# A two-layer decoder trunk on one core: fewer VectorE steps in GELU, softmax coefficients and gate norm, and another plan of the order

## The chip, the core and the metric

The kernel runs on one core of one Trainium2 chip. The core has a matrix engine (TensorE, PE in the profile, its weight loads PEld), three engines for elementwise work (VectorE = DVE, ScalarE = ACT, GpSimd = POOL), a queue that starts transfers (SyncE = SP), and 16 DMA engines between the chip's memory (HBM) and the core's own. The metric is the device time of one launch in microseconds, the median of several runs; lower is better.

## What is computed

One sequence of 512 tokens, width 1024, passes through two layers. Each mixes the tokens by three head groups side by side and adds a feed-forward; all modulated by a conditioning vector c:

```python
for l in range(DEPTH):
    mod = (silu(c) @ w_ada[l] + b_ada[l])[:, None, :]
    sh1, sc1, g1, sh2, sc2, g2 = jnp.split(mod, 6, axis=-1)
    h = x * (1.0 + sc1) + sh1
    (hq, hf, hi, hg, nq, kcm, vcm, ksl, vsl, kwn, vwn, ngt, gu, gv) = jnp.split(h @ w_in[l], cuts, axis=-1)
    o_h = hgrn2(...)          # a gated recurrence in chunks of 64
    o_n = nsa(...)            # sparse attention: compressed, selected and window part
    o_g = gmlp(gu, gv, ...)   # gelu(gu) * (tril(w_s) @ LN(gelu(gv)) + b_s)
    mix = jnp.concatenate([o_h, o_n, o_g], axis=-1) @ w_o[l]
    x = layer_norm(DN_ALPHA * x + (1.0 + g1) * mix, ln1_w[l], ln1_b[l])
    h = x * (1.0 + sc2) + sh2
    y = jnp.square(jax.nn.relu(h @ w_ff1[l])) @ w_ff2[l]
    x = layer_norm(DN_ALPHA * x + (1.0 + g2) * y, ln2_w[l], ln2_b[l])
# attention: out = g0 * softmax(cmp) @ v_cmp + g1 * softmax(slc) @ v_slc + g2 * softmax(win) @ v_win
# gelu(x) = 0.5 x (1 + tanh(sqrt(2/pi) (x + 0.044715 x^3)))
```

## The kernel before

Matrix products keep float32 accuracy by splitting each operand into a high part and a residual: `whi` and `wlo` of a weight piece `wraw`, `hT` and `aT` in pairs of the activations, three matmuls for one product. The residual `wlo` can be made by VectorE or GpSimd.

The program goes through eight stages. Layer 0's mixing lasts from 0 to about 347 us: the conditioning products (`adaw`, summed on VectorE into `adacc`, turned into columns by `ada_cols` or rows), the input projections, the recurrence (`hq`, `hog`, states `hst`), the compression of keys and values (`KV` copies, a small network with GELU into `chid`), the attention in eight units of 128 queries and four heads, the gMLP, the output projection. Then layer 0's feed-forward to about 727 us, layer 1's mixing to about 1021, its feed-forward to about 1387, and a tail with the last layer norm.

In an attention unit (`att_unit`) each of four heads has three score parts. VectorE takes the negated row maximum (`amax`), ScalarE the exponential with its row sum, VectorE the reciprocal of the sums times the gates (`acoef`, 128 rows by four heads by three parts), then the probabilities `P` are scaled (`scale_rows`: GpSimd, VectorE or ScalarE), transposed on TensorE into the bank `aps`, and copied as a high part and a residual `PT`. The projections of `hi`, `hg`, `gv` and `gu` run between the units. `gelu2` is used by the compression (four tiles of 62 rows, source in PSUM) and by `ev_gu` and `ev_gv` (eight tiles of 128x256 in each). `ev_gv` also does the gMLP's norm, with statistics `gst`, `gmv` and rows of weights `gnw`; its two halves go to `gmv[k]`. `final_rows` makes the last residual: `rt` from a bank, `y` = `rt` + `base`, then statistics `lnst`, and at the end `xs`, the normed rows.

The code does not run in the order in which it is written. Every call on `V`, `A`, `G`, `PE` or `SP` makes an operation in a `Plan`, some with alternatives: `vg` names VectorE first and GpSimd second, `gv` the other way. `schedule` then places all operations by a list scheduler (`place_all`): at each step an engine takes the ready operation of the best priority. Durations come from `cost`, distances between engines from `LAT`. An alternative that is not the first is taken only when the operation has been ready for `ALT_WAIT` ns. After each round, `latest(order)` works the priorities out of the latest starts of the order just found; the order with the earliest modelled end is emitted. Since operations are emitted from one line, that line carries all the instructions in the profile, and tiles tell them apart.

Of the kernel before, what the change touches and what calls it, by code (L numbers as in the profile page):

```python
# [161 lines left out]
ALT_WAIT = 500.0  # L162
# [5 lines left out]
ROUNDS = 6  # L168
# [28 lines left out]
class Plan:  # L197
# [158 lines left out]
    def schedule(self, rounds=ROUNDS):  # L356
# [16 lines left out]
        for r in range(rounds):  # L373
            if r:
                self.latest(order)
                reset()
            order = self.place_all()
            end = max(o.end for o, _ in order)
            if best is None or end < best[0]:
                best = (end, order, [(vt, vt.slot) for vt in tiles])  # L380
# [43 lines left out]
    def place_all(self):  # L424
# [90 lines left out]
        while n_left:  # L515
            best = None
            for e in T:
# [14 lines left out]
                for r in sorted(ready[e])[:200]:  # L532
# [4 lines left out]
                    if r[2] and t < o.ready + ALT_WAIT:  # L537
                        fut = min(fut, max(st, o.ready + ALT_WAIT))
# [12 lines left out]
                if cand is None:  # L551
                    for r in pend[e]:
# [5 lines left out]
                        fut = min(fut, max(r[0] + (ALT_WAIT if r[2] else 0), slot_time(o, r[0]), bank_time(o, e),  # L558
# [13 lines left out]
            c = self.cost(*alt)  # L572
# [112 lines left out]
def trunk(ctx: ExitStack, tc: tile.TileContext, I, out, depth=L):  # L685
# [362 lines left out]
    def ada_cols(l, v, c0, acc, dst):  # L1048

        nb = acc.shape[1] // 128  # L1050
        p = ps()[:, :nb * 128]
# [111 lines left out]
    def layer(l, yn, xd, sb1, rest, mods):  # L1163
# [235 lines left out]
        def gelu2(dst, src, n, tag):  # L1399
# [4 lines left out]
            A.activation(a, src, AF.Square)  # L1404
            V.tensor_scalar(a, a, 0.044715, 1.0, op0=OP.mult, op1=OP.add)
            (V.tensor_mul if src.vt.cls == "ps" else lambda *z: vg("tensor_mul", *z))(a, a, src)
# [100 lines left out]
        def ev_gv(j, p):  # L1507
# [9 lines left out]
            V.tensor_scalar(ge, ge, mv[:, 0:1], mv[:, 2:3], op0=OP.subtract, op1=OP.mult)  # L1517
            vg("tensor_mul", ge, ge, gnw[:, 0])
            for k in range(2):
                vg("tensor_add", gmv[k][:, j], ge[:, k * 128:(k + 1) * 128], gnw[:, 1, k * 128:(k + 1) * 128])  # L1520
# [12 lines left out]
        def att_unit(g, i):  # L1533
# [5 lines left out]
            for h in range(4):  # L1539
# [26 lines left out]
                srcs = (p0[:, n0 - n:n0], p1[:, :n], pcm)  # L1566
                for m in range(3):
                    V.tensor_reduce(nm[:, h, m:m + 1], srcs[m], axis=AX.X, op=OP.max, negate=True)
                dsts = (Pt[0][:, :n], Pt[1][:, :n], Pc[:, h])
# [4 lines left out]
            cf = small([128, 4, 3], "acoef", 4)  # L1574
            V.reciprocal(cf, sm)
            gt = gates[:, i, 12 * g:12 * g + 12].rearrange("p (h m) -> p h m", m=3)
            V.tensor_mul(cf[:, :, 0:1], cf[:, :, 0:1], gt[:, :, 1:2])
            V.tensor_mul(cf[:, :, 1:2], cf[:, :, 1:2], gt[:, :, 2:3])
            V.tensor_mul(cf[:, :, 2:3], cf[:, :, 2:3], gt[:, :, 0:1])
            if i == 0:  # L1580
                V.tensor_scalar(cf[:, :, 2:3], cf[:, :, 2:3], cvalid, None, op0=OP.mult)
            for h in range(4):
                for m in range(2):
                    scale_rows(Ps[h][m][:, :n], cf[:, h, m:m + 1])
# [381 lines left out]
```

## Time and profile before

| | us |
|---|---|
| median of 3 runs | 1399.25 |
| lowest, highest | 1399.09, 1402.97 |
| the profiled execution | 1398.26 |
| its span, first to last instruction | 1396.5 |
| TensorE busy | 1346.9 (96%) |
| VectorE busy | 1051.6 (75%) |
| ScalarE busy | 580.2 (42%) |
| GpSimd busy | 428.5 (31%) |

Times of single instructions are of the profiled execution. Busy time of an engine counts its instructions; its idle time before an instruction is put down to what ended it. A row that stands for several instructions gives their count (x16) and the mean of one. The granted clock of TensorE is 0.993 of full speed in the mean of the span.

### The profile page before, as it was taken

The page shows a single profiled execution, that of the slowest core. Times are in us where ns is not written, and L with a number is a line of the kernel's source. Part 1 is how long each engine was busy: PE and PEld are TensorE (multiplying, and loading weights), DVE is VectorE, ACT ScalarE, POOL GpSimd, SP SyncE. Part 2 cuts the span into 40 slices and gives each one's busy share as a digit, 9 for nine tenths or more (in the row PEclk, how much of TensorE's full clock was granted, in tenths as well). Part 3 has the DMA queues.
Part 4 walks back from the last instruction along what each step waited for, and adds up shares of the span by engine and source line. Part 5 has one row for each costly group of instructions (what it writes and reads, how often), then busy time and mean ns, then how long its engine had stood idle before and what let it go on. Part 6 is the DMA issues. An engine that isn't in the chain of part 4 may idle for free.

```text
span 1396.5 us, 21252 instructions
## 1 busy us (share of the span) xinstructions
PE 1346.9 (96%) x7339; PEld 1124.7 (81%) x7339; DVE 1051.6 (75%) x2242; ACT 580.2 (42%) x1570; POOL 428.5 (31%) x623
## 2 busy tenths in 40 slices
PE   5998999989999999999999999999999999999997
PEld 4887788868888888888889878888788888888886
DVE  8997799989786495585888957988995448634567
ACT  6567587862343133211325467876333102210121
POOL 6685345582210000000224632336530000000024
PEclk9999999999999999999999999999999999999999
DMA  9734634136564294283503351112643235413431
GB/s 308 231 99 123 208 105 143 46 108 199 169 207 156 83 320 140 92 290 123 166 1 108 110 174 44 31 46 91 212 133 100 90 96 170 149 39 109 125 113 61
DMA packets 119844, 185.67 MB, mean 133 GB/s; under 512 B 9796, under 2 KB 47160, under 8 KB 119736
## 3 DMA queue, kind: packets, MB, share of 16 engines
q1 hardware_dynamic: 119736, 184.31, 41.9%
q8 instruction: 58, 0.95, 0.3%
q14 instruction: 50, 0.41, 0.1%
HBM read 175.89 MB, written 8.39 MB: 132 GB/s over the span
## 4 chain that ended last, share of the span: by engine, by line
PE 75%; DVE 12%; ACT 4%; DMA 4%; issue 2%; POOL 2%; SPq 1%; POOLq 0%; DVEq 0%; ACTq 0%
PE acc L681 64%; PE aps L681 7%; PE ps L681 5%; DMA adaw<-in_w_ada_dram 2%; DVE adacc L681 1%; DMA adaq<-in_w_ada_dram 1%; DVE amax L681 1%; DMA wraw<-in_w_in_dram 1%; DVE ge L681 1%; ACT P L681 1%; ACT KV L681 1%; DVE PT L681 1%; SPq L681 1%; DVE r L681 1%; DVE rt L681 1%
## 5 line engine op out<-in xcount | busy, mean ns | idle before, releaser
L681 PE MATMUL acc<-hT,whi 128*128 128x512 f32 (+1 forms) x1296 | 414.7, 374 | 3.8 <-ACT hT L681 3.5
L681 POOL TENSOR_TENSOR wlo<-wraw,whi 128x256 fp32r<-128x256 f32 (+2 forms) x133 | 152.6, 1158 | 612.9 <-ACT whi L681 533.3
L681 PE MATMUL acc<-whi,aT 128*128 128x512 f32 x896 | 325.1, 394 | 0.0
L681 PEld LDWEIGHTS acc<-hT,whi 128*128 128x128 f32 x1296 | 235.4, 190 | 49.4 <-ACT hT L681 4.3
L681 PE MATMUL acc<-hT,wlo 128*128 128x512 f32 (+1 forms) x648 | 239.6, 372 | 0.1
L681 PE MATMUL acc<-whi,hT 128*128 128x256 f32 (+2 forms) x1024 | 230.2, 308 | 3.3 <-ACT KV L681 2.5
L681 PEld LDWEIGHTS acc<-whi,aT 128*128 128x128 f32 x896 | 168.2, 188 | 39.5
L681 DVE TENSOR_TENSOR wlo<-wraw,whi 128x512 fp32r<-128x512 f32 (+2 forms) x267 | 182.7, 700 | 13.6 <-ACT whi L681 6.4
L681 ACT ACTIVATE ffa<-acc 128x512 f32<-128x512 f32 x64 | 38.1, 596 | 372.1 <-PE acc L681 371.1
L681 ACT ACTIVATE whi<-wraw 128x512 fp32r<-128x512 f32 (+2 forms) x253 | 131.3, 556 | 120.1 <-DMA wraw<-in_w_ff_dram 71.8
L681 PEld LDWEIGHTS acc<-whi,hT 128*128 128x128 f32 x1024 | 169.7, 191 | 11.2 <-ACT KV L681 3.5
L681 PE MATMUL acc<-wlo,aT 128*128 128x512 f32 x448 | 176.8, 395 | 0.0
L681 PE MATMUL acc<-wlo,hT 128*128 128x256 f32 (+2 forms) x512 | 156.2, 306 | 0.4 <-DVE wlo L681 0.4
L681 DVE TENSOR_TENSOR ffs<-ffa 128x512 f32<-128x512 f32 x64 | 46.7, 732 | 141.4 <-ACT ffa L681 141.3
L681 PEld LDWEIGHTS acc<-hT,wlo 128*128 128x128 f32 x648 | 123.1, 190 | 23.0 <-DVE wlo L681 0.5
L681 DVE SCALAR_TENSOR_TENSOR adacc<-adaw,silc,adacc 128x512 f32<-128x512 f32 x140 | 113.8, 823 | 15.4 <-DMA adaw<-in_w_ada_dram 13.8
L681 PEld LDWEIGHTS acc<-wlo,hT 128*128 128x128 f32 x512 | 97.6, 191 | 3.4 <-DVE wlo L681 0.6
L681 PEld LDWEIGHTS acc<-wlo,aT 128*128 128x128 f32 x448 | 84.1, 188 | 19.6
L681 ACT ACTIVATE P<-aps,amax 128x128 f32<-128x128 f32 (+3 forms) x128 | 66.9, 530 | 14.3 <-DVE amax L681 12.2
L681 DVE TENSOR_REDUCE amax<-aps 128x1 f32<-128x32 f32 (+4 forms) x192 | 65.4, 379 | 8.5 <-PE aps L681 7.6
L681 DVE CAST whi<-wraw 128x512 fp32r<-128x512 f32 (+1 forms) x147 | 59.6, 407 | 1.3 <-DMA wraw<-in_w_ff_dram 1.1
L681 PE MATMUL aps<-PT,Vt 128*128 128x512 f32 x160 | 51.4, 414 | 3.8 <-DVE PT L681 3.1
(315 smaller groups left out, 2307.7 us busy)
## 6 DMA issues: line engine op xcount, KB each, us to landing
wraw<-in_w_ff_dram SPq DMA_DIRECT2D x128, 512.0 KB, 4.6
adaw<-in_w_ada_dram SPq DMA_DIRECT2D x80, 512.0 KB, 5.1
wraw<-in_w_in_dram SPq DMA_DIRECT2D x49, 256.0 KB, 3.1
adaq<-in_w_ada_dram SPq DMA_DIRECT2D x32, 256.0 KB, 5.9
wraw<-in_w_o_dram SPq DMA_DIRECT2D x16, 512.0 KB, 3.8
wraw<-in_w_in_dram SPq DMA_DIRECT2D x15, 512.0 KB, 3.9
xd<-xs SPq DMA_DIRECT2D x24, 256.0 KB, 2.5
xr<-xd SPq DMA_DIRECT2D x24, 256.0 KB, 4.7
```

The lines of the kernel that those rows point to most:

```text
L681: getattr(self.handles[e], method)(*a, **k)
```

## The change

In the computation: `gelu2` puts the factor 0.044715 into the square on ScalarE (as the root, in its scale), and does `(a + 1) * src` in one VectorE instruction where there were a scalar step and a multiplication. The gate norm becomes `(ge - mean) * w` and, for each half, `* rstd + b`, three two-input VectorE instructions with no alternative on GpSimd. The score parts of the attention are numbered in the order of the gates, so that one multiplication of 128x12 replaces three of 128x4. `ada_cols` of layer 0 sums over partitions by a matmul with a column of ones and one add, where it transposed and reduced. The last `y` is put on VectorE.

In the planner: one more round, the wait for an alternative set by round, from the fifth round on (r > 3) the priorities taken from the best order so far, and 1.1 times the duration for each operation that is not on TensorE or SP.

```diff
-ALT_WAIT = 500.0
-ROUNDS = 6
+ROUNDS = 7
+ALT_WAITS = (500.0, 500.0, 500.0, 500.0, 0.0, 250.0, 1000.0)
+SLACK = 1.1
...
-                self.latest(order)
+                self.latest(best[1] if r > 3 else order)
                 reset()
+            self.alt_wait = ALT_WAITS[r]
...
-                    if r[2] and t < o.ready + ALT_WAIT:
+                    if r[2] and t < o.ready + self.alt_wait:
...
-            c = self.cost(*alt)
+            c = self.cost(*alt) * (1.0 if e in ("PE", "SP") else SLACK)
...
     def ada_cols(l, v, c0, acc, dst):
         nb = acc.shape[1] // 128
+        if l == 0:
+            p = ps()[:, :nb]
+            for b in range(nb):
+                PE.matmul(p[:, b:b + 1], acc[:, b * 128:(b + 1) * 128], ones[:, 0:1], start=True, stop=True)
+            V.tensor_add(dst, p, bada[:, l, v, c0 // 128:c0 // 128 + nb])
+            return
...
-            A.activation(a, src, AF.Square)
-            V.tensor_scalar(a, a, 0.044715, 1.0, op0=OP.mult, op1=OP.add)
-            (V.tensor_mul if src.vt.cls == "ps" else lambda *z: vg("tensor_mul", *z))(a, a, src)
+            A.activation(a, src, AF.Square, scale=math.sqrt(0.044715))
+            V.scalar_tensor_tensor(a, a, 1.0, src, op0=OP.add, op1=OP.mult)
             A.activation(a, a, AF.Tanh, scale=math.sqrt(2.0 / math.pi))
             V.scalar_tensor_tensor(dst, a, 1.0, src, op0=OP.add, op1=OP.mult)
...
-            V.tensor_scalar(ge, ge, mv[:, 0:1], mv[:, 2:3], op0=OP.subtract, op1=OP.mult)
-            vg("tensor_mul", ge, ge, gnw[:, 0])
+            V.scalar_tensor_tensor(ge, ge, mv[:, 0:1], gnw[:, 0], op0=OP.subtract, op1=OP.mult)
             for k in range(2):
-                vg("tensor_add", gmv[k][:, j], ge[:, k * 128:(k + 1) * 128], gnw[:, 1, k * 128:(k + 1) * 128])
+                kc_ = slice(k * 128, (k + 1) * 128)
+                V.scalar_tensor_tensor(gmv[k][:, j], ge[:, kc_], mv[:, 2:3], gnw[:, 1, kc_], op0=OP.mult, op1=OP.add)
...
-                srcs = (p0[:, n0 - n:n0], p1[:, :n], pcm)
+                srcs = (pcm, p0[:, n0 - n:n0], p1[:, :n])
...
-            V.tensor_mul(cf[:, :, 0:1], cf[:, :, 0:1], gt[:, :, 1:2])
-            V.tensor_mul(cf[:, :, 1:2], cf[:, :, 1:2], gt[:, :, 2:3])
-            V.tensor_mul(cf[:, :, 2:3], cf[:, :, 2:3], gt[:, :, 0:1])
+            V.tensor_mul(cf, cf, gt)
...
-            vg("tensor_add", d[1][:, c], t, bases[j][:, c])
+            V.tensor_add(d[1][:, c], t, bases[j][:, c])
```

What the plan makes of it is shown at three places. In a row of the order stand the line, the operation, out<-in and the shape; a number behind a name tells its tiles apart.

VectorE at the end of the attention of layer 0, before. `PT` are the residuals of the last transposed probabilities, for which TensorE waits; `ge` and `gel` belong to GELU and gate norm, `gmv` and `gnw` to the norm:

```order
L681 CAST PT_4236<-aps_4175 128x512
L681 TENSOR_TENSOR PT_4242<-aps_4173,PT_4232 128x512
L681 TENSOR_TENSOR PT_4247<-aps_4196,PT_4239 128x512
L681 TENSOR_TENSOR PT_4255<-aps_4175,PT_4236 128x512
L681 TENSOR_TENSOR PT_4258<-aps_4187,PT_4244 128x512
L681 TENSOR_SCALAR ge_4194<-ge_4194,gmv_1_4210 128x256
L681 TENSOR_TENSOR ge_4194<-ge_4194,gnw_1999 128x256
L681 TENSOR_SCALAR gel_4160<-gel_4160 128x256
L681 TENSOR_TENSOR PT_4288<-aps_4267,PT_4276 128x512
L681 TENSOR_SCALAR gel_4165<-gel_4165 128x256
L681 TENSOR_TENSOR PT_4301<-aps_4274,PT_4290 128x512
L681 TENSOR_TENSOR PT_4309<-aps_4285,PT_4296 128x512
```

The same place now; `hog` is the recurrence's output, `pcT` the compressed part's probabilities:

```order
L683 TENSOR_TENSOR PT_4141<-aps_4081,PT_4126 128x512
L683 TENSOR_TENSOR PT_4150<-aps_4086,PT_4135 128x512
L683 TENSOR_TENSOR PT_4158<-aps_4097,PT_4144 128x512
L683 TENSOR_TENSOR hog_4169<-ps_4069,hms_4131 128x256
L683 TENSOR_TENSOR PT_4174<-aps_4083,PT_4147 128x512
L683 TENSOR_TENSOR PT_4188<-aps_4129,PT_4154 128x512
L683 TENSOR_TENSOR PT_4198<-aps_4160,PT_4176 128x512
L683 TENSOR_TENSOR PT_4209<-aps_4088,PT_4162 128x512
L683 TENSOR_TENSOR PT_4221<-aps_4179,PT_4196 128x512
L683 TENSOR_TENSOR pcT_2102<-aps_4200,pcT_2082 32x128 x4
```

Steps of gate norm and GELU stood between the PT; they stand behind them now.

VectorE at the recurrence's output of layer 1, where TensorE waits for `hog` (`hms` its mean square, `hst` the state), before:

```order
L681 SCALAR_TENSOR_TENSOR hst_11555<-hst_11560,hft_8448,ps_11707 64x64
L681 TENSOR_SCALAR ge_11619<-ge_11619,gmv_1_11658 128x256
L681 TENSOR_SCALAR ge_11627<-ge_11627,gmv_0_11691 128x256
L681 TENSOR_REDUCE hms_11768<-hsq_11764 128x4
L681 TENSOR_TENSOR ge_11619<-ge_11619,gnw_9480 128x256
L681 TENSOR_TENSOR hog_11774<-ps_11715,hms_11742 128x256
L681 TENSOR_TENSOR gmv_11726<-ge_11619,gnw_9480 128x128
L681 TENSOR_TENSOR gmv_11726<-ge_11627,gnw_9480 128x128
L681 TENSOR_TENSOR hog_11774<-hog_11774,hgg_10725 128x256
L681 TENSOR_REDUCE hms_11790<-hsq_11783 128x4
L681 TENSOR_TENSOR gmv_11745<-ge_11494,gnw_9480 128x128
L681 TENSOR_TENSOR hog_11799<-ps_11733,hms_11768 128x256
```

The same place now:

```order
L683 SCALAR_TENSOR_TENSOR ge_11541<-ge_11541,gmv_0_11686,gnw_9388 128x256
L683 TENSOR_TENSOR hog_11724<-ps_11653,hms_11691 128x256
L683 TENSOR_REDUCE hms_11734<-hsq_11730 128x4
L683 TENSOR_TENSOR hog_11739<-ps_11674,hms_11711 128x256
L683 TENSOR_TENSOR hog_11724<-hog_11724,hgg_10711 128x256
L683 SCALAR_TENSOR_TENSOR ge_11593<-ge_11593,gmv_1_11718,gnw_9388 128x256
L683 SCALAR_TENSOR_TENSOR gmv_11625<-ge_11541,gmv_0_11686,gnw_9388 128x128
L683 TENSOR_TENSOR hog_11764<-ps_11704,hms_11734 128x256
```

Between the first hog made from a bank (`ps`) and the next such stood five rows, three of them the gate norm's; now one row stands there, and the gate norm's rows come behind the second.

ScalarE at the eviction of the key and value projections of layer 0, before. `krope`, `Vt`, `KhS` and `KV` are the copies of keys and values out of a bank (`acc` or `ps`), `hbd` is the recurrence's, `whi` a weight's high part:

```order
L681 ACTIVATE whi_1615<-wraw_1495 128x280
L681 ACTIVATE Vt_1620<-acc_1264 128x2x64
L681 ACTIVATE krope_1626<-acc_1361 128x128
L681 ACTIVATE Vt_1632<-acc_1361 128x2x64
L681 ACTIVATE KV_1_1570<-ps_1622 64x128 x2
L681 ACTIVATE KV_75_1575<-ps_1622 64x128 x2
L681 ACTIVATE KV_37_1578<-ps_1622 64x128 x2
L681 ACTIVATE KV_46_1581<-ps_1622 64x128 x2
L681 ACTIVATE whi_1664<-wraw_1495 128x280
L681 ACTIVATE hbd_845<-hgq_940 64x4x64 x2
L681 ACTIVATE hbd_848<-hgq_952 64x4x64 x2
```

The same place now, from the first such copy out of the four banks acc on; the 32 KV follow behind it, 24 of them as x2 rows, with a KhS after each eight to sixteen:

```order
L683 ACTIVATE krope_1513<-acc_1153 128x128
L683 ACTIVATE krope_1516<-acc_1138 128x128
L683 ACTIVATE Vt_1521<-acc_1138 128x2x64
L683 ACTIVATE Vt_1525<-acc_1211 128x2x64
L683 ACTIVATE krope_1528<-acc_1211 128x128
L683 ACTIVATE Vt_1530<-acc_1153 128x2x64
L683 ACTIVATE krope_1534<-acc_1238 128x128
L683 ACTIVATE Vt_1541<-acc_1238 128x2x64
L683 ACTIVATE whi_1547<-wraw_1498 128x280
L683 ACTIVATE whi_1550<-wraw_1498 128x280
L683 ACTIVATE hbd_824<-hgq_919 64x4x64 x2
L683 ACTIVATE hbd_827<-hgq_934 64x4x64 x2
```

The copies out of all four banks `acc` stand in one row now, with all the KV behind them, where the KV were mixed with `hbd`, `whi`, `krope` and `Vt` before.

## Rows read from the trace of the kernel before

**Rows 1.** the page's part 1: busy us of each engine, share of span, instructions
```profile
PE 1346.9 (96%) x7339; PEld 1124.7 (81%) x7339; DVE 1051.6 (75%) x2242; ACT 580.2 (42%) x1570; POOL 428.5 (31%) x623
```

**Rows 2.** busy time by stretch: length, then each engine's us (instructions), PE clock, DMA
```profile
250.00:300.00 50.00, 44.75 (x280) 35.04 (x279) 46.81 (x106) 40.02 (x113) 36.73 (x52) 0.99 0.23 70
...
950.00:1000.00 50.00, 46.41 (x281) 39.61 (x280) 45.41 (x92) 27.05 (x68) 34.16 (x45) 1.00 0.42 136
...
1200.00:1250.00 50.00, 50.00 (x218) 40.49 (x216) 26.03 (x45) 8.24 (x14) 1.82 (x1) 1.00 0.31 95
```

**Rows 3.** TensorE's waits, whole span: tile, what ended them, us total, times, longest
```profile
PE aps L681 <- DVE PT L681: 3.1, 3, 1.5
...
PE ps L681 <- DVE hog L681: 2.5, 3, 1.2
...
PE acc L681 <- ACT KV L681: 2.5, 2, 2.3
...
PE ps L681 <- DVE amax L681: 1.8, 1, 1.8
...
PE aps L681 <- POOL P L681: 1.1, 2, 0.7
...
PE aps L681 <- DVE P L681: 0.7, 2, 0.4
```

**Rows 4.** groups of instructions by form: busy us, mean ns, idle before and releaser
```profile
L681 DVE TENSOR_TENSOR acoef<-acoef,gates 128x4 f32<-128x4 f32 x48 | 8.6, 193 | 0.2
...
L681 DVE TENSOR_REDUCE adat<-ps 128x4 f32<-128x512 f32 x12 | 8.2, 687 | 9.0 <-PE ps L681 8.9
...
L681 DVE SCALAR_TENSOR_TENSOR ge<-gel,gx 128x256 f32<-128x256 f32 x16 | 13.1, 845 | 0.5 <-ACT gel L681 0.5
...
L681 DVE TENSOR_SCALAR gel<-gel 128x256 f32<-128x256 f32 x16 | 6.6, 426 | 0.0
...
L681 DVE TENSOR_TENSOR gel<-gel,gx 128x256 f32<-128x256 f32 x7 | 4.3, 619 | 0.1
...
L681 DVE TENSOR_SCALAR ge<-ge,gmv 128x256 f32<-128x256 f32 x8 | 4.7, 597 | 0.1
...
L681 DVE TENSOR_TENSOR ge<-ge,gnw 128x256 f32<-128x256 f32 x4 | 3.2, 794 | 0.0
...
L681 DVE TENSOR_TENSOR gmv<-ge,gnw 128x128 f32<-128x128 f32 x5 | 2.1, 432 | 0.0
...
L681 DVE SCALAR_TENSOR_TENSOR adacc<-adaq,silc,adacc 128x128 f32<-128x128 f32 x14 | 7.1, 508 | 0.4
```

**Rows 5.** one operation's durations: min/median/max ns, first and last start us
```profile
L681 DVE SCALAR_TENSOR_TENSOR ge<-gel,gx x16: 411/552/1529, 253.0 to 987.9; 128x256 f32<-128x256 f32 x16
```

**Rows 6.** VectorE in order of time, end of attention of layer 0
```profile
290.04 1.13 DVE L681 TENSOR_SCALAR ge<-ge,gmv 128x256 f32<-128x256 f32 x1
...
291.20 1.38 DVE L681 TENSOR_TENSOR ge<-ge,gnw 128x256 f32<-128x256 f32 x1
...
292.50 0.28 DVE L681 TENSOR_SCALAR gel<-gel 128x256 f32<-128x256 f32 x1
```

**Rows 7.** VectorE in order of time, compression of layer 0
```profile
160.78 0.75 DVE L681 SCALAR_TENSOR_TENSOR adacc<-adaw,silc,adacc 128x512 f32<-128x512 f32 x1 [2.39 <-DMA adaw<-in_w_ada_dram]
```

**Rows 8.** all engines in order of time, end of the program
```profile
1387.56 0.41 DVE L681 TENSOR_TENSOR rt<-acc,grow 128x256 f32<-128x256 f32 x1
...
1387.90 0.73 DVE L681 SCALAR_TENSOR_TENSOR xs<-xs,lnmv,lnb 128x512 f32<-128x512 f32 x1
...
1388.05 1.16 POOL L681 TENSOR_TENSOR y<-rt,base 128x256 f32<-128x256 f32 x1 [1.65 <-DVE rt L681]
...
1389.25 0.43 DVE L681 BATCH_NORM_STATS2 lnst<-y 128x6 f32<-128x256 f32 x1 [0.62 <-POOL y L681]
```

**Rows 9.** ScalarE's KV group, then one TensorE row of layer 0's projections
```profile
L681 ACT ACTIVATE KV<-ps 64x128 f32<-64x128 f32 x56 | 15.2, 271 | 2.4 <-PE ps L681 1.7
...
124.84 0.51 PE L681 MATMUL acc<-whi,hT 128*128 128x280 f32 x1 [2.29 <-ACT KV L681]
```

More of the change, by code (lines that the diff above doesn't have):

```diff
@@ L536, in place_all @@
                     st = max(slot_time(o, t), bank_time(o, e), port_time(o, r[2], e))
-                    if r[2] and t < o.ready + ALT_WAIT:
-                        fut = min(fut, max(st, o.ready + ALT_WAIT))
+                    if r[2] and t < o.ready + self.alt_wait:
+                        fut = min(fut, max(st, o.ready + self.alt_wait))
                         continue
@@ L557, in place_all @@
                             continue
-                        fut = min(fut, max(r[0] + (ALT_WAIT if r[2] else 0), slot_time(o, r[0]), bank_time(o, e),
+                        fut = min(fut, max(r[0] + (self.alt_wait if r[2] else 0), slot_time(o, r[0]), bank_time(o, e),
                                            port_time(o, r[2], e)))
@@ L1565, in att_unit @@
                 PE.matmul(p1[:, n - 128:n], identb, mneg, start=False, stop=True)
[L1566 removed]
+                srcs = (pcm, p0[:, n0 - n:n0], p1[:, :n])
                 for m in range(3):
                     V.tensor_reduce(nm[:, h, m:m + 1], srcs[m], axis=AX.X, op=OP.max, negate=True)
[L1569 removed]
+                dsts = (Pc[:, h], Pt[0][:, :n], Pt[1][:, :n])
                 for m in range(3):
@@ L1574, in att_unit @@
             cf = small([128, 4, 3], "acoef", 4)
+            gt = gates[:, i, 12 * g:12 * g + 12].rearrange("p (h m) -> p h m", m=3)
             V.reciprocal(cf, sm)
-            gt = gates[:, i, 12 * g:12 * g + 12].rearrange("p (h m) -> p h m", m=3)
-            V.tensor_mul(cf[:, :, 0:1], cf[:, :, 0:1], gt[:, :, 1:2])
-            V.tensor_mul(cf[:, :, 1:2], cf[:, :, 1:2], gt[:, :, 2:3])
-            V.tensor_mul(cf[:, :, 2:3], cf[:, :, 2:3], gt[:, :, 0:1])
+            V.tensor_mul(cf, cf, gt)
             if i == 0:
-                V.tensor_scalar(cf[:, :, 2:3], cf[:, :, 2:3], cvalid, None, op0=OP.mult)
+                V.tensor_scalar(cf[:, :, 0:1], cf[:, :, 0:1], cvalid, None, op0=OP.mult)
             for h in range(4):
                 for m in range(2):
-                    scale_rows(Ps[h][m][:, :n], cf[:, h, m:m + 1])
-            gv("tensor_mul", Pc, Pc, cf[:, :, 2:3].to_broadcast([128, 4, 32]))
+                    scale_rows(Ps[h][m][:, :n], cf[:, h, m + 1:m + 2])
+            gv("tensor_mul", Pc, Pc, cf[:, :, 0:1].to_broadcast([128, 4, 32]))
             po = ps(name="aps")
```

## Prediction

> **What bounds the kernel now.** I read the busy times first. TensorE is busy for 1346.9 us of a span of 1396.5, VectorE for 1051.6 [rows 1]. So at most about 50 us can be won without removing matmuls. Then the stretches, to see where those 50 us lie. In the feed-forward, TensorE is busy 50.00 of 50 us and VectorE 26.03: a VectorE instruction there is worth nothing. At the end of the attention of the first layer TensorE has 44.75 of 50 and VectorE 46.81, and at the same place of the second layer 46.41 and 45.41 [rows 2]. There VectorE is as full as TensorE, and its steps can hold TensorE up. Last the waits of TensorE by what ended them, and what VectorE did just then. Of the waits on steps near the change, TensorE waits 3.1 us for PT, 2.5 for hog, 2.5 for KV (a ScalarE copy), 1.8 for amax, and 1.1 and 0.7 for a scaled P [rows 3]. They sum to 11.7 us, under 1% of the time. The rest of the 50 us is the start, the tail, and many small waits.
>
> **The change part by part.** All sums are made against the profiled run, 1398.26 us (span 1396.5, 1.76 around it); it is 0.99 under the median of 1399.25, and I add that back at the end.
>
> *VectorE's work, before asking where it counts.* The coefficients lose 32 of 48 multiplications at 193 ns: -6.2 us. Column sums of layer 0 lose four reductions at 687 ns and gain four adds of a 128x4 tile, at most 193 ns each as the coefficient step of that size: -2.7 + 0.8 = -1.9. Sixteen transposes on TensorE become sixteen matmuls of one column: equal count, taken as nothing. GELU loses a scalar step (16 at 426 ns, 6.6 us, and at most the same price for the four of 62 rows, 1.7) and a multiplication, of which VectorE had 7 of 16 (4.3 us); it gains 16 two-input steps, for which the nearest row is the last step of the same GELU, 845 ns in the mean: 13.5. Net +0.9 on VectorE. Gate norm loses 4.7, 3.2 and 2.1 us and gains 8 x 0.845 = 6.8 and 16 half-width steps; the nearest row of that width and kind is 508 ns: 8.1. Net +4.9 [rows 4]. So the two "savings" that look largest in the diff put work onto VectorE, since 9 of the 16 multiplications of GELU and 15 of the 24 instructions that follow the gate norm's first ran on GpSimd before. The final adds put about 1 us more on it (1.16 on GpSimd for the last [rows 8]). Sum: -6.2 - 1.9 + 0.9 + 4.9 + 1 = -1.3. VectorE does fewer steps and not less work.
>
> That rests on the 845 ns. The same step took 411 ns at the quickest and 1529 at the longest [rows 5], and at 411 GELU would come to 6.6 - 12.6 = -6.0 and the gate norm, with its halves at the 432 ns of the adds before [rows 4], to 3.3 + 6.9 - 10.0 = +0.2, so VectorE would do some 13 us less. In front of PT a two-input step took 1.38 us, 3.4 times that quickest one [rows 6]. The Trainium skill, "SBUF — State Buffer", section "Who interferes with whom", says that a VectorE instruction with two SBUF inputs contends with a GpSimd instruction that reads SBUF, the one that comes first holding the shared ports. By it the new steps are stretched where GpSimd is busy and all others are relieved, since GpSimd has fewer instructions now; with all stretching gone VectorE's sum would be the lower one. The spread of that step agrees with the rule, and does not show which of the two engines pays.
>
> *Order.* The larger part of the change is the planner: more rounds, waits of 0 to 1000 before the second engine of an alternative is taken, and 10% added to the time of every VectorE, ScalarE and GpSimd step. The plan moves 31 of the 512-wide weight residuals from GpSimd to VectorE (a two-input step of that size took 0.73 us [rows 8], so 23 us). I cost them at nothing: most are in the feed-forward, where VectorE has over 20 us idle of 50. Without that cover each would cost up to its 0.73.
>
> *End of attention, layer 0.* TensorE waits 3.1 us for PT. In front of the two late PT stand a 1.13, a 1.38 and a 0.28 us step of gate norm and GELU [rows 6]. In the new order nine PT stand together, with one hog step among them, and GELU comes behind. I take -3 (bounds -3.1 and 0). Next late there are the copies to PT on ScalarE, a smaller wait.
>
> *Hog, layer 1.* 2.5 us of waits [rows 3]; two or three gate-norm steps leave the rows between one hog and the next. -1.5 (0 to -2.5).
>
> *Coefficients.* Two multiplications of 193 ns [rows 4] leave the front of each of 16 units: 0.386 per unit. TensorE waits four times for P, 1.8 us in all [rows 3], so 4 x 0.386 = -1.5; other units pass some of it on through GpSimd, at most 0.5. -2 (0 to -2).
>
> *Chid and amax.* The wait of 1.8 stays: VectorE itself stands idle 2.39 us for the adaw transfer with an adacc, and amax is queued behind that [rows 7]. A step less in front: -0.4.
>
> *Tail.* Pinning the final add spares GpSimd's 1.16 us, and VectorE would wait 0.62 less [rows 8]. But in the new order VectorE has an xs step between rt and y, another between y and the statistics, and two between the statistics and what GpSimd needs from them. By the plain times, with 0.73 for such a step [rows 8] less what overlaps, the end moves by some 1 us: +1 (-0.6 to +1.5).
>
> *Copies KV, layer 0.* The new plan finishes the four key and value banks together, so 32 KV copies at 271 ns stand in one row on ScalarE with only KhS among them: 8.7 us. Before, other work stood between them, and TensorE waited 2.3 us for one of them here [rows 9]. It has some 16 matmuls to do meanwhile. I take +1 (-2.3 to +7).
>
> *Reserve on the rest.* No row prices a plan with reserve. It removes scattered waits in the two mixing stages and may make others, since TensorE's own order changes too. About 50 - 12 us is outside the waits above, the start and the tail included; I take -2, with bounds of -10 and +6.
>
> Sum: -3 - 1.5 - 2 - 0.4 + 1 + 1 - 2 = -6.9, so 1391.4 for a run like the profiled one, and 1392 against the median.
>
> **Rivals.** *No change.* VectorE does the same amount of work, and what leaves the front of one PT or hog stands in front of something else; the feed-forward, half of the time, cannot gain. For: VectorE's sum of -1.3 us, and that each wait that goes is under 3.5 us. Against: the rows that hold up PT are moved behind all of it. Then -3 + 1 + 1 = -1, and with the 0.99, 1398.3.
>
> *Slower by the KV copies.* TensorE runs out of matmuls while ScalarE copies four banks in a row. Three waits like the one of 2.3 us [rows 9] in place of one, and a fourth at the next bank, would be +6.9 over the sum without gains: 1398.3 + 6.9 = 1405. It decides from the point where the 16 matmuls are done before two of the four banks are copied, 16 x 0.271 = 4.3 us; if they last longer, it costs nothing. For: the copies alone are 8.7 us. Against: ScalarE is busy only 42% of the span [rows 1], and a plan with reserve allows 10% more for just these copies.
>
> *Larger gain.* The 24 instructions of GELU and gate norm that have left GpSimd no longer run beside VectorE's, the two-input steps take 411 in place of 845 ns, and VectorE does 13 us less in the two tight stages; a third of that ends up on TensorE, and the reserve takes 8 in place of 2. Then -6.9 - 4.3 - 6 = -17.2, so 1382 against the median. The rule of the Trainium skill on the shared ports, above, points this way. Against: the new steps have two inputs themselves, and GpSimd keeps weight work in these stages.
>
> *The change does less than it says* is the first rival: fewer steps, no shorter time.
>
> **How the numbers follow.** My forecast has a chance of 0.50, no change 0.28, slower 0.13, larger gain 0.09. 0.3%, 4.2 us, is about what a measurement of this kernel can tell from no change. Faster than 1395.05: nearly all of the forecast (0.46), and the larger gain: 0.55. Slower than 1403.4: the KV case, 0.13, and a little for a reserve that ends badly: 0.15. The rest, 0.30, lies between. The range runs from 1382, the forecast with the reserve at -10, the hog waits gone and the tail at its lower bound (-8 - 1 - 1.6, rounded), to 1402, no change with the KV copies at half of their upper bound; it leaves out the slower case and half of the larger gain. The forecast alone has 1386 to 1397.
>
> **What would show it.** In the profile after: TensorE's wait for PT under 0.5 us and the stretch of the end of attention at over 47 us busy; waits for hog under 1.5; amax still about 1.5; KV under 3.5 (above 6 the slower rival); VectorE's busy time within 15 us of 1051.6 and GpSimd's lower by more than that; from the last rt to the end of the span 9 to 10.5 us, against 8.9 [rows 1, 8]. The GELU step at 500 to 850 ns shows which end of its bound holds. The forecast is wrong if TensorE's busy time changes by more than 5 us, or if new waits above 2 us stand anywhere outside the start.

## The result

The changed kernel takes 1380.65 us (median of 4 runs, 1379.14 to 1383.58) where the kernel before takes 1399.17; the ratio is 0.9866, with a 95% interval of 0.9847 to 0.9884. That is 18.5 us, more than twice the 7 us that were forecast, and 1.35 us under the lower end of the stated range. The profiled run took 1380.88 us, its span is 1379.2.

The page of the changed kernel, busy time and its chain of work that ended last:

```profile
span 1379.2 us, 21123 instructions
PE 1337.6 (97%) x7355; PEld 1125.0 (82%) x7355; DVE 1026.6 (74%) x2226; ACT 596.5 (43%) x1597; POOL 338.6 (25%) x548
...
PE 89%; ACT 3%; DVE 3%; DMA 2%; POOL 1%; issue 1%; SPq 1%; POOLq 0%; ACTq 0%; DVEq 0%
```

Against [rows 1] VectorE is busy 25.0 us less, GpSimd 89.9 us less and ScalarE 16.3 us more. TensorE is busy 9.3 us less and idle 8.0 us less (49.6 us before, 41.6 now). Where the time went is seen by the place at which each stage's matmuls stand. TensorE in order of time, of the kernel before, the first scores of layer 0's attention and its last product with the values (start, duration):

```profile
142.04 0.34 PE L681 MATMUL aps<-KhW,qs 128*128 128x128 f32 x2
...
297.32 0.50 PE L681 MATMUL aps<-PT,Vt 128*128 128x512 f32 x1 [0.23 <-DVE PT L681]
```

The same two places of the changed kernel:

```profile
141.36 0.56 PE L683 MATMUL aps<-KhW,qs 128*128 128x128 f32 x4
...
283.87 0.48 PE L683 MATMUL aps<-PT,Vt 128*128 128x512 f32 x1
```

From the one to the other it took 155.8 us to the end of the last product before, and 143.0 now (283.87 + 0.48 - 141.36). Not all of these 12.8 us are won there, as the stages one by one show. First before: the attention of layer 0, the rest of its mixing (to the last matmul with `mixT`, the output projection's input), its feed-forward, and the whole mixing of layer 1 (columns as in [rows 2]):

```profile
142.04:297.82 155.78, 147.89 (x1023) 121.91 (x1022) 138.44 (x362) 113.28 (x387) 81.44 (x128) 1.00 0.39 118
297.82:353.80 55.98, 54.41 (x262) 44.01 (x262) 52.37 (x101) 19.64 (x48) 23.51 (x27) 0.97 0.58 192
353.80:719.30 365.50, 365.39 (x1682) 299.74 (x1682) 257.81 (x430) 97.74 (x179) 39.60 (x32) 1.00 0.50 163
719.30:1028.00 308.70, 299.84 (x2005) 258.93 (x2004) 258.53 (x662) 184.75 (x586) 145.54 (x218) 1.00 0.33 100
```

The same four of the changed kernel:

```profile
141.36:284.35 142.99, 141.64 (x1017) 119.67 (x1016) 125.59 (x332) 112.96 (x386) 62.90 (x101) 1.00 0.39 119
284.35:342.20 57.85, 56.77 (x286) 46.70 (x285) 53.32 (x106) 21.99 (x54) 25.34 (x29) 1.00 0.55 177
342.20:707.20 365.00, 365.00 (x1683) 299.69 (x1682) 258.92 (x452) 99.81 (x182) 20.97 (x23) 1.00 0.52 168
707.20:1010.00 302.80, 296.35 (x2006) 259.02 (x2005) 250.89 (x627) 191.11 (x601) 126.21 (x201) 0.99 0.33 100
```

In the attention TensorE's idle time falls from 7.9 to 1.4 us. The rest of the 12.8 is busy time, and part of that only moved: twelve matmuls with `mixT`, 3.8 us, stood inside this stretch before and stand behind it now, so 1.9 us are given back in the rest of the mixing. All in all layer 0's mixing ends 11.6 us sooner (353.8, now 342.2), layer 1's mixing is 5.9 us shorter, most of it at its end, the two feed-forwards give under 1 us together, as they had to, and the tail is 1.0 us longer. The ends of matmuls are modelled in the profile, so busy time can contain short waits; how much of the 9.3 us is that isn't shown. The stretch that [rows 2] showed for the end of the attention:

```profile
250.00:300.00 50.00, 48.30 (x326) 40.55 (x326) 45.41 (x108) 38.57 (x106) 29.47 (x43) 1.00 0.23 74
```

TensorE goes from 44.75 to 48.30 us [rows 2], with VectorE still at 45.41. What TensorE waits for, whole span, those that answer to [rows 3] and the new ones of the key and value projections:

```profile
PE ps L683 <- DVE hog L683: 3.2, 2, 2.5
...
PE ps L683 <- ACT krope L683: 1.8, 2, 0.9
PE ps L683 <- POOL krope L683: 1.6, 2, 0.9
...
PE ps L683 <- ACT KV L683: 1.1, 1, 1.1
PE aps L683 <- DVE PT L683: 1.0, 2, 0.6
...
PE ps L683 <- DVE chid L683: 0.3, 1, 0.3
...
PE aps L683 <- ACT P L683: 0.2, 1, 0.2
```

PT fell from 3.1 to 1.0, a P scaled by VectorE or GpSimd from 1.8 to nothing, amax (1.8) is gone. Hog is no better than before: 3.2 us after 2.5, and one of its waits now lasts 2.5. And the steps that the diff touches, by form (answers to [rows 4]):

```profile
L683 DVE SCALAR_TENSOR_TENSOR gel<-gel,gx 128x256 f32<-128x256 f32 x16 | 11.6, 753 | 0.1
L683 DVE SCALAR_TENSOR_TENSOR ge<-gel,gx 128x256 f32<-128x256 f32 x16 | 10.8, 708 | 0.1
L683 DVE SCALAR_TENSOR_TENSOR gmv<-ge,gmv,gnw 128x128 f32<-128x128 f32 x16 | 9.7, 622 | 0.1
...
L683 DVE SCALAR_TENSOR_TENSOR ge<-ge,gmv,gnw 128x256 f32<-128x256 f32 x8 | 4.6, 585 | 0.1
...
L683 DVE TENSOR_TENSOR acoef<-acoef,gates 128x12 f32<-128x12 f32 x16 | 3.1, 193 | 0.1
```

### The profile page after: what moved, and what is told of

The parts are those of the page before. It is cut to its first block, busy times and chain, and to the rows that moved or that the text cites. A ratio compares the mean times of both kernels' runs of the same rounds, so it can differ in the third digit from the quotient of the medians.

```text
span 1379.2 us, 21123 instructions
## 1 busy us (share of the span) xinstructions
PE 1337.6 (97%) x7355; PEld 1125.0 (82%) x7355; DVE 1026.6 (74%) x2226; ACT 596.5 (43%) x1597; POOL 338.6 (25%) x548
## 4 chain that ended last, share of the span: by engine, by line
PE 89%; ACT 3%; DVE 3%; DMA 2%; POOL 1%; issue 1%; SPq 1%; POOLq 0%; ACTq 0%; DVEq 0%
PE acc L683 73%; PE aps L683 9%; PE ps L683 6%; SPq L683 1%; DMA wraw<-in_w_in_dram 1%; ACT KV L683 1%; ACT P L683 1%; DMA x<-in_x_dram 0%; DMA adaq<-in_w_ada_dram 0%; DMA adaw<-in_w_ada_dram 0%; POOL adacc L683 0%; DVE xs L683 0%; DVE ge L683 0%; POOL hms L683 0%; DVE gel L683 0%
## 5 line engine op out<-in xcount | busy, mean ns | idle before, releaser
L683 PE MATMUL acc<-whi,hT 128*128 128x256 f32 (+2 forms) x1024 | 225.8, 307 | 0.0
L683 DVE TENSOR_TENSOR wlo<-wraw,whi 128x512 fp32r<-128x512 f32 (+2 forms) x313 | 201.7, 662 | 11.5 <-ACT whi L683 5.6
L683 ACT ACTIVATE whi<-wraw 128x512 fp32r<-128x512 f32 (+2 forms) x261 | 135.1, 558 | 126.4 <-DMA wraw<-in_w_ff_dram 65.8
L683 PE MATMUL acc<-wlo,hT 128*128 128x256 f32 (+2 forms) x512 | 155.8, 305 | 0.0
L683 POOL TENSOR_TENSOR wlo<-wraw,whi 128x256 fp32r<-128x256 f32 (+2 forms) x87 | 90.0, 1039 | 183.6 <-ACT whi L683 79.0
L683 DVE SCALAR_TENSOR_TENSOR adacc<-adaw,silc,adacc 128x512 f32<-128x512 f32 x140 | 108.2, 783 | 13.9 <-DMA adaw<-in_w_ada_dram 12.6
L683 POOL TENSOR_TENSOR base<-y,grow 128x512 f32<-128x512 f32 x2 | 3.4, 1682 | 299.3 <-DVE y L683 299.3
L683 ACT ACTIVATE P<-aps,amax 128x512 f32<-128x512 f32 (+3 forms) x128 | 67.0, 530 | 10.5 <-DVE amax L683 9.3
L683 DVE TENSOR_TENSOR PT<-aps,PT 128x512 fp32r<-128x512 f32 x80 | 51.6, 683 | 8.0 <-ACT PT L683 6.2
```

Source lines behind the costliest of these rows:

```text
L683: getattr(self.handles[e], method)(*a, **k)
```

## Experiments

Ratios are to runs of the kernel before on the same chip. All kernels that plan anew have other orders than the changed kernel, those marked "order kept" have its order (or that of e1, where it says so), instruction by instruction.

| kernel | median us | ratio | 95% interval |
|---|---|---|---|
| changed kernel | 1380.65 | 0.9866 | 0.9847 to 0.9884 |
| edits, planner of before (e1) | 1394.16 | 0.9972 | 0.9958 to 0.9985 |
| computation of before, new planner (e2) | 1405.39 | 1.0048 | 1.0033 to 1.0063 |
| changed, reserve off (e3) | 1398.03 | 0.9990 | 0.9974 to 1.0005 |
| order kept, steps split again (e4) | 1384.93 | 0.9911 | 0.9889 to 0.9932 |
| changed, six rounds (e5) | 1398.60 | 1.0005 | 0.9995 to 1.0015 |
| changed, 5% and 19 rounds (e6) | 1392.06 | 0.9958 | 0.9940 to 0.9977 |
| e1's order kept, steps split (e7) | 1401.56 | 1.0018 | 1.0003 to 1.0034 |
| order kept, more on GpSimd (e8) | 1392.20 | 0.9955 | 0.9943 to 0.9966 |
| an order of a longer search (e9) | 1380.61 | 0.9887 | 0.9868 to 0.9906 |
| a second one (e11) | 1378.97 | 0.9874 | 0.9858 to 0.9891 |
| computation of before, longer search (e10) | 1399.31 | 1.0023 | 1.0008 to 1.0038 |
| order kept, coefficients split (e12) | 1379.25 | 0.9884 | 0.9867 to 0.9901 |
| without the GELU edit, planned anew (e13) | 1389.25 | 0.9923 | 0.9905 to 0.9941 |
| without the gate-norm edit | 1385.49 | 0.9893 | 0.9879 to 0.9908 |
| without the column-sum edit | 1380.43 | 0.9861 | 0.9843 to 0.9879 |
| without the coefficient edit | 1389.16 | 0.9929 | 0.9907 to 0.9952 |

### Edits or planner

The first theory (P) was that the planner brings the gain, the rival (S) that the fewer steps do. One kernel has the edits and the old planner:

```diff
-ROUNDS = 7
+ROUNDS = 6
-ALT_WAITS = (500.0, 500.0, 500.0, 500.0, 0.0, 250.0, 1000.0)
+ALT_WAITS = (500.0,) * 6
-SLACK = 1.1
+SLACK = 1.0
...
-                self.latest(best[1] if r > 3 else order)
+                self.latest(order)
```

> The changed computation (GELU, coefficients, gate norm, column sums, final add), planned as before: 6 rounds, wait 500, priorities from the last order, no reserve. Theory P (the planner's reserve and its rounds bring the 18.5 us): 1393 to 1401. Theory S (fewer VectorE steps and less beside them on GpSimd bring it): 1379 to 1386.

The second has the computation of before and the planner of after (the planner's part of the diff alone):

> The computation as before, planned as after the change: 7 rounds, waits by round, priorities from the best order, times of VectorE, ScalarE and GpSimd times 1.1. Theory P: 1379 to 1388. Theory S: 1393 to 1401. If both e1 and e2 gain about half, 1388 to 1393 each, the two add up.

The third is the changed kernel with one number set back:

```diff
-SLACK = 1.1
+SLACK = 1.0
```

> The changed kernel with the reserve of 1.1 set back to 1.0, all else as after the change. If the reserve is what the planner's part is worth (theory P): 1392 to 1400, with TensorE's small waits in the attention of layer 0 back. If rounds and waits do it, or the steps (theory S): 1379 to 1385.

Neither theory holds for all three. The edits alone (1394.16) and the changed kernel without reserve (1398.03) lie where P put them, but the planner alone (1405.39) lies above the ranges of both. The edits alone gain 0.3%, the planner alone loses 0.5%, and the two together gain 1.3%: they are worth more than their sum. Without the reserve the changed kernel is where the kernel before is.

The planner's loss has a rival in TensorE's clock, which the traces show granted at full or at half speed. Its mean in the four executions of e2 is 0.984 to 0.987 of full speed. In the profiled one it falls right behind the attention of layer 0, in whose last 6 us TensorE waited five times, for PT and pcT. From 300 to 350 us it is 0.86 there, where the kernel before has 0.98 and the changed kernel 1.00:

```profile
300.00:350.00 50.00, 46.12 (x209) 37.61 (x209) 35.89 (x76) 14.86 (x34) 13.31 (x15) 0.86 0.49 157
```

The kernel before has 0.991 to 0.997 on this chip, but for two executions at 0.984 and 0.986, and these took 1407.84 and 1407.08 us. So at such a clock e2 is no slower than the kernel before, and it isn't shown that its order would lose anything at the usual one. That the two are worth more than their sum holds without this loss too: with the planner alone put at nothing, 0.3% stands against 1.3%.

### Is it the seventh round, and how large a reserve

```diff
-ROUNDS = 7
+ROUNDS = 6
```

> The changed kernel with reserve, but without the seventh round (the one with a wait of 1000 for the second engine): the order emitted is that of the second round, whose end in the planner, reserve included, is 1388.4 us against 1365.4 for the seventh. Theory Q (the reserve alone is worth nothing; the time follows the planned end with the reserve in it, which the changed kernel's measured time exceeds by 15 us): 1398 to 1406. Theory R (any order planned with the reserve gains, since its steps tolerate delays): 1381 to 1390.

Theory R falls and Q's range is met: with the reserve, but with an order whose planned end is 23 us later, nothing is gained. Part of what is missing may again be the clock, 0.987 to 0.991 in these ten executions; the four of the kernel before on record at 0.984 to 0.988 took 1401 to 1408. In the next, the reserve is halved and the rounds are 19, with waits of 300 to 3000 in the further ones.

```diff
-ROUNDS = 7
+ROUNDS = 19
-SLACK = 1.1
+SLACK = 1.05
```

> The changed computation with a reserve of 5% and 19 rounds; planned end, reserve included, 1359.1 us. Without a reserve the measured time lay 37 to 41 us over the planned end, with 10% 13 to 15. Theory Q, half way between: 1359 + 27 = 1386, 1380 to 1391. If only a reserve of 10% helps: 1394 or more. If the end planned decides whatever the reserve: 1375 or less.

1392.1 lies in none of the three ranges, just above that of Q: 5% gives a third of the gain, although GpSimd is busy for 266.8 us only in that kernel, less than in any other. So a low load of GpSimd is not the cause by itself.

### Is it one lucky order

The same planner ran on with the reserve of 10%, noise on its priorities and other waits, some 300 rounds from two seeds for the changed computation and some 330 for the old one. The best orders were written into the kernels as tables; the diff is the table and the lines that read it, in place of the rounds:

```diff
-        for r in range(rounds):
-            if r:
...
+        order = array.array("H", zlib.decompress(base64.b85decode(ORDER)))
+        return [(self.ops[v // 4], v % 4) for v in order]
```

> The changed computation with an order found by some 300 further rounds of the same planner (reserve of 10%, waits of 300 to 2000, priorities of the better orders with noise added), written into the kernel as a table. Its planned end, reserve included, is 1360.4 us, 5.0 under that of the changed kernel. Theory Q (measured time = planned end with the reserve + some 15 us): 1375, 1372 to 1379, faster than both kernels. Theory L (the order of the changed kernel is a lucky one, and the planned end says nothing): anywhere between 1381 and 1400, as for the other orders.

> A second such order, from other random numbers, planned end with reserve 1360.9 us. Theory Q: 1376, 1373 to 1380, within 3 us of the first. Theory L: 1381 to 1400 and unlike the first.

> The computation before the change with the best order of some 330 rounds with the reserve of 10%; its planned end, reserve included, is 1384.9, since the old steps leave VectorE and GpSimd less room. Theory Q: 1384.9 + 15 = 1400, 1396 to 1404; no gain over the kernel before, however long one looks, which would say that the reserve pays only with the fewer steps. If a longer search with a reserve is the whole gain: 1376 to 1386.

The two found orders come out at the time of the changed kernel, within their intervals. So that one is no lucky find: three orders planned with the reserve to a planned end of 1360 to 1365 us take 1379 to 1381. But of the 5 us that the planned end falls further nothing is to be seen in the ratios (the first order lies above Q's range, the second inside it); none of the kernels here is shown to be faster than the changed one. The old computation with the reserve stays at 1399 after some 330 rounds, and not for the clock: its five executions at 0.992 or more took 1397.1 to 1399.3. Its busy times are these:

```profile
PE 1348.3 (96%) x7339; PEld 1127.8 (81%) x7339; DVE 1029.4 (74%) x2269; ACT 593.5 (42%) x1592; POOL 361.8 (26%) x574
```

Over the span VectorE and GpSimd are relieved nearly as much as in the changed kernel, and nothing is gained by it. In the attention of layer 0 they are not: this is its row, and below it that of the edits with the old planner (e1); the changed kernel's, with 125.59 and 62.90, stands above.

```profile
143.73:307.10 163.37, 153.85 (x1038) 126.02 (x1036) 138.71 (x372) 120.79 (x403) 84.52 (x128) 0.99 0.39 121
...
141.14:288.77 147.63, 143.28 (x1009) 119.43 (x1008) 129.50 (x343) 108.32 (x373) 58.42 (x93) 1.00 0.39 119
```

TensorE's waits in its attention of layer 0 (columns as in [rows 3]):

```profile
PE aps L666 <- DVE PT L666: 4.6, 7, 2.1
PE aps L666 <- ACT P L666: 1.9, 2, 1.2
PE ps L666 <- DVE hog L666: 1.6, 1, 1.6
```

and in the same stretch of the second found order of the changed computation, where these three are all that is listed:

```profile
PE ps L666 <- DVE hog L666: 1.6, 2, 1.1
PE ps L666 <- DVE gog L666: 1.3, 1, 1.3
PE ps L666 <- DVE hst L666: 0.6, 1, 0.6
```

Seven waits for PT in the one, none in the other: in the order found for the fewer steps TensorE does not wait for the probabilities, in the one found for the old steps it does.

### What the steps cost in a fixed order

The order is kept, and the fused steps of GELU, of the gate norm's first half and of the coefficients are emitted as separate ones again at their place, 60 instructions more, in the changed kernel (e4) and in the order of the edits without reserve (e7):

```diff
+            if e == "V" and method == "scalar_tensor_tensor" and nm == "gel":
+                h.tensor_scalar(a[0], a[1], a[2], None, op0=k["op0"])
+                h.tensor_mul(a[0], a[0], a[3])
+            elif e == "V" and method == "scalar_tensor_tensor" and nm == "ge" and k["op0"] == OP.subtract:
+                h.tensor_scalar(a[0], a[1], a[2], None, op0=OP.subtract)
+                h.tensor_mul(a[0], a[0], a[3])
+            elif e == "V" and method == "tensor_mul" and nm == "acoef":
+                for m in range(3):
+                    h.tensor_mul(a[0][:, :, m:m + 1], a[1][:, :, m:m + 1], a[2][:, :, m:m + 1])
```

> The order of the changed kernel kept, instruction by instruction, but each fused VectorE step emitted as the separate steps again at its place: GELU 20 scalar steps more, gate norm 8 more, coefficients 32 multiplications of 128x4 more, some 15 us of VectorE's busy time. Theory P: at most 3 us over the changed kernel, 1380 to 1384. Theory S: 1388 to 1396.

> The order of the edits planned without reserve (measured 1394.2), kept, with the fused steps emitted as separate ones again: the same 60 small VectorE steps more that cost 4.3 us in the changed kernel's order. Theory R (a plan with reserve tolerates delays, one without does not): +8 to +15, 1402 to 1409. If the orders are equally sensitive: +3 to +6, 1397 to 1400.

The ratio rises by 0.0045 in the first (0.9866 to 0.9911) and by 0.0046 in the second (0.9972 to 1.0018), 6 us each by these ratios. Both medians lie between the ranges of the two theories. Theory R, that a plan with reserve bears delays better, is not borne out: the order with reserve looks as sensitive as the one without, though by the intervals a difference of some 5 us would not show. In these fixed orders the steps are thus worth about a third of the gain. With the coefficients alone split (the last three lines):

> The changed kernel's order kept, only the 32 coefficient multiplications of 128x4 back (three for one in each attention unit, 0.39 us in front of each unit's probabilities). If they stand on the path of TensorE's waits for P as forecast: +1.5 to +2, 1382 to 1383. If covered: 0. If they are most of the 4.3 us that all the split steps cost: +3 to +4.

the ratio is 0.9884 and overlaps that of the changed kernel: they cost nothing that the runs can show.

### Room on GpSimd

```diff
             getattr(self.handles[e], method)(*a, **k)
+            out = o.alts[ai][2][0] if o.alts[ai][2] else None
+            nm = out.vt.name if isinstance(out, VA) else ""
+            if e == "V" and method == "scalar_tensor_tensor" and nm in ("gel", "ge") or nm[:3] == "gmv" and e == "V" and method == "scalar_tensor_tensor":
...
+                self.handles["G"].tensor_mul(self.scr, self.scr, self.scr)
```

> The changed kernel's order kept, and behind each of the 60 two-input VectorE steps of GELU and gate norm one multiplication of 128x256 on GpSimd on a scratch tile that nobody reads: some 44 us more of GpSimd in the two tight stages. Theory C (the gain is VectorE freed from GpSimd's accesses): 1386 to 1396, with VectorE's two-input steps stretched. Theory Q: GpSimd has room, 1381 to 1385.

It costs 12 us (ratio 0.9955), so GpSimd has no room in these stages. VectorE's waits in the attention of layer 0 and up to 350 us, changed kernel:

```profile
DVE hog L683 <- POOL hms L683: 1.6, 3, 0.6
```

and with the added work:

```profile
DVE hog L684 <- POOL hms L684: 4.2, 4, 1.7
```

The power of the mean square, `hms`, is on GpSimd behind what was added, `hog` waits for it, and TensorE waits more for `hog` (3.2 us before) and for `gog`, the gMLP's output, of which no wait was listed. Whole span, with the added work:

```profile
PE ps L684 <- DVE hog L684: 5.6, 3, 4.6
PE ps L684 <- DVE gog L684: 4.0, 2, 2.6
```

And VectorE is stretched, unevenly (min/median/max ns of the two two-input steps of GELU, with the added work):

```profile
L684 DVE SCALAR_TENSOR_TENSOR gel<-gel,gx x16: 409/426/1532, 251.3 to 982.0; 128x256 f32<-128x256 f32 x16
L684 DVE SCALAR_TENSOR_TENSOR ge<-gel,gx x16: 404/830/1517, 260.8 to 988.1; 128x256 f32<-128x256 f32 x16
```

The second had a median of 416 in the changed kernel. But VectorE's busy time over the span rises by 5.5 us only (1026.6 to 1032.1), GpSimd's by 40.8. So the stretch can hardly be all of the 12 us; the exact shares of queue and stretch, and with them theory C, stay open.

### Which edit makes the room

Each kernel takes one edit back to the lines of before and plans anew with the reserve (the best of 100 rounds, as a table).

> The changed computation without the GELU edit, with the best order of 100 rounds with the reserve (planned end 1368.7; all edits: 1361.3 to 1365.4 of 95 rounds; none: 1385.4). If this edit carries the gain: 1394 or more. If each of the edits carries a part of it, as the planned ends say: 1382 to 1388.

> The same without the gate-norm edit (planned end 1365.7). If this edit carries the gain: 1394 or more. If the parts add up: 1379 to 1385.

> The same without the column-sum edit of layer 0 (planned end 1364.6). If this edit carries the gain: 1394 or more. If the parts add up: 1379 to 1385.

> The same without the coefficient edit (planned end 1369.3). If this edit carries the gain, by what the planner can do with it rather than by its place in the changed kernel's order: 1394 or more. If the parts add up: 1382 to 1388.

No median reaches 1394, so no edit carries it alone. Three of the four lie just above the ranges for parts that add up, the column sums inside theirs. Against the changed kernel's 0.9866, the ratio is 0.0057 higher without GELU's edit and 0.0063 without the coefficients', some 8 and 9 us; 0.0027 without the gate norm's, where the intervals overlap; and no higher without the column sums. Each is one order of a search, and three orders of one computation differed by 0.0021 above, so the first two are shown, by one order each, and the third is not. The coefficients are the plainest case: in a fixed order their 32 multiplications cost little or nothing, but the plan that had to fit them in with a reserve came out 9 us later.

The nine orders with 10% of reserve whose planned end is on record fall into three groups by it. Ends of 1360.4 to 1365.7 us were measured at 1379.0 to 1385.5, ends of 1368.7 and 1369.3 at 1389.2, ends of 1384.9 and 1388.4 at 1399.3 and 1398.6.

## Why the prediction was wrong

*The sign and the places were right.* The gain is in the two mixing stages, layer 0's above all, and the feed-forward gives next to nothing although 31 more weight residuals stand on VectorE.

*Work of VectorE.* The coefficients went from 48 to 16 multiplications of 193 ns, 9.3 to 3.1 us (forecast -6.2). The gate norm takes 4.6 + 9.7 = 14.3 us where 10.0 stood, +4.3 (forecast +4.9). GELU's new step takes 753 ns against the 845 assumed. So these terms held, and the busy time still fell by 25.0 us, outside the 15 that were allowed. A part is work that the planner moved: copies of PT on VectorE went from 16 to 5 and on ScalarE from 64 to 75, which was to be seen in the order beforehand and was not priced.

```profile
L683 ACT ACTIVATE PT<-aps x75: 580/599/666, 169.2 to 941.4; 128x512 fp32r<-128x512 f32 x75
L683 DVE CAST PT<-aps x5: 680/691/692, 224.6 to 920.2; 128x512 fp32r<-128x512 f32 x5
```

But moved work goes both ways, and the 31 residuals alone put more on VectorE than these copies took off. What is left is that the same steps take less time. The groups that stand equally often in both traces are 1498 instructions of VectorE, and in sum they take 26.7 us less; 1006 such instructions of ScalarE take 0.2 us less. One of these groups, before and after:

```profile
L681 DVE SCALAR_TENSOR_TENSOR adacc<-adaw,silc,adacc 128x512 f32<-128x512 f32 x140 | 113.8, 823 | 15.4 <-DMA adaw<-in_w_ada_dram 13.8
L683 DVE SCALAR_TENSOR_TENSOR adacc<-adaw,silc,adacc 128x512 f32<-128x512 f32 x140 | 108.2, 783 | 13.9 <-DMA adaw<-in_w_ada_dram 12.6
```

GpSimd is busy 89.9 us less meanwhile, and the other runs go with it. The same comparison with the kernel before gives 44 us less for the 5% order (GpSimd 266.8 us), 30 for the old computation after its long search (361.8), and 4 to 8 for e1, e2, e3 and e5, where GpSimd is busy for 410 to 486.

*Column sums.* The forecast took TensorE's part as equal. Sixteen transposes, 2.5 us in the attention of layer 0, became 32 recorded matmuls of one column, 3.9 us, so this put 1.4 us on TensorE.

*Single waits.* End of attention: forecast -3, the waits for PT fell by 2.1. Coefficients: forecast -2, the waits for P fell from 1.8 to 0 on VectorE's and GpSimd's side, with 0.2 left on ScalarE's; but with the multiplications split again the kernel is no slower, so this term was luck as far as the runs can tell. Chid and amax: forecast -0.4, the wait for amax of 1.8 became one for chid of 0.3. Amax still stands behind the transfer, as forecast, but VectorE waited 1.20 us for that instead of 2.39 [rows 7]:

```profile
159.44 0.75 DVE L683 SCALAR_TENSOR_TENSOR adacc<-adaw,silc,adacc 128x512 f32<-128x512 f32 x1 [1.20 <-DMA adaw<-in_w_ada_dram]
160.10 0.28 DVE L683 TENSOR_REDUCE amax<-aps 128x1 f32<-128x128 f32 x1
```

so what this term won is mostly the shorter wait for the transfer and not the step that is gone. Hog: forecast -1.5, it is 3.2 after 2.5, wrong; VectorE there waits for GpSimd's `hms`, 3.4 us in six waits in the whole span, which the chosen rows did not show:

```profile
956.93 0.42 DVE L683 TENSOR_TENSOR hog<-ps,hms 128x256 f32<-128x256 f32 x1 [0.58 <-POOL hms L683]
...
958.45 0.42 DVE L683 TENSOR_TENSOR hog<-ps,hms 128x256 f32<-128x256 f32 x1 [0.57 <-POOL hms L683]
```

*Tail.* Forecast +1; from the end of the last matmul to the end of the span it is 10.5 us (1368.66 to 1379.2) after 9.6 (1386.95 to 1396.5). From the last rt, the forecast's own measure, it is 10.5 after 8.9 [rows 8], +1.6 and just beyond the bound of +1.5. The xs stand where they were said to stand:

```profile
1368.69 0.42 DVE L683 TENSOR_TENSOR rt<-acc,grow 128x256 f32<-128x256 f32 x1 [0.24 <-PE acc L683]
1369.04 0.74 DVE L683 SCALAR_TENSOR_TENSOR xs<-y,lnmv,lnw 128x512 f32<-128x512 f32 x1
1369.70 0.42 DVE L683 TENSOR_TENSOR y<-rt,base 128x256 f32<-128x256 f32 x1
1370.03 0.74 DVE L683 SCALAR_TENSOR_TENSOR xs<-y,lnmv,lnw 128x512 f32<-128x512 f32 x1
```

*KV.* Forecast +1, with a slower rival. The wait for KV went from 2.5 to 1.1, waits for krope of 3.4 came, and the attention starts 0.7 us sooner. The rival did not happen.

*Signs against the forecast.* Two that it had named came true: TensorE's busy time changed by 9.3 us, where 5 was the limit, and a new wait above 2 us stands outside the start, 2.5 us for hog in layer 1:

```profile
959.26 0.44 PE L683 MATMUL ps<-ident,hog 128*128 128x128 f32 x2 [2.55 <-DVE hog L683]
```

*The step that failed* is "reserve on the rest", put at -2 with bounds of -10 and +6. The forecast's other terms sum to -4.9 and the profiled run is 17.4 us shorter, so with the others as forecast this term was some -12.5, beyond its bound. Three things were wrong in it. It was priced as a term of its own, added to those of the edits, and the runs show that it isn't one: the planner without the edits is +0.5%, the edits without the planner -0.3%, together -1.3%. The waits that the profile names were taken for most of what there was to win, and this term for a remainder: TensorE's listed waits from 130 to 350 us fell from 8.9 to 2.1 us, while layer 0's mixing ends 11.6 us sooner. And TensorE's busy time was taken as fixed (what can be won was bounded by the 50 us outside it, and a change above 5 us counted as a sign against the forecast), whereas 9.3 of the 17.3 us of span came out of it, with 16 more matmuls on record.

*The rival "larger gain"* gave the time, 1382, and had 0.09. That is not its mechanism confirmed. Its relief of VectorE is there, and larger than its 13 us: VectorE does 25.0 us less over the span, and the last GELU step went from a mean of 845 ns to 708 (median 552 [rows 5], now 416), though the new steps did not come down to 411 (753 in the mean). But relief over the span doesn't bring the gain by itself: the old computation after its long search has it too and stays at 1399, and with 5% of reserve GpSimd did still less and only a third of the gain came. The rule that the prediction took from the Trainium skill, "SBUF — State Buffer", section "Who interferes with whom", agrees with what the added work on GpSimd did to the second GELU step (median 416 to 830 ns) and not with the first (419 to 426).

What is argued and not shown: that the plan spends as its reserve the room which the edits make on VectorE and GpSimd. The room itself is measured. In the attention of layer 0 VectorE went from 138.44 to 125.59 us and GpSimd from 81.44 to 62.90, and the stage became shorter by as much, so that VectorE is as full as before (88% after 89%). The edits without reserve have most of this room (129.50 and 58.42) in 147.6 us, the reserve without the edits has none of it (138.71 and 84.52) in 163.4.

What stays open: why 10% gives so much more than 5%, and what makes up the fall of TensorE's busy time.

## What to carry to other kernels

Price a planner's change together with the edits it comes with: run each alone before adding terms, since a reserve that costs time on a full engine can pay once some steps are gone. A few short steps that cost nothing at their place in one order can cost several us when the whole is planned anew around them, so an experiment that only puts them back in the old order does not give their worth. Bound what a new order can win neither by the named waits nor by TensorE's idle time: here more than half of the gain came out of its busy time. And look at the granted clock of each execution before a loss of half a percent is put down to an order.

## What the runs showed of the hardware

Sixty multiplications of 128x256 on GpSimd on a tile that nothing else touches, 604 to 1062 ns each, made the kernel 12 us slower, though no step of the kernel reads or writes that tile:

```profile
L691 POOL TENSOR_TENSOR scr<-scr x60: 604/638/1062, 146.4 to 993.0; 128x256 f32<-128x256 f32 x60
```

The two-input VectorE steps of 128x256 of GELU take from 404 to 1532 ns in that run, 3.8 times.

The same VectorE instructions take less time in traces where GpSimd is busy for less: 1498 of them 26.7 us less with 338.6 us of GpSimd in place of 428.5, while ScalarE's keep theirs.

Two executions of the kernel before at a mean granted clock of 0.984 and 0.986 took 1407.84 and 1407.08 us, where the median on that chip was 1398.74.
